# Block sums behind the low parts of probabilities, a wider spread of two of the sums, and one FFN sum on VectorE

## The chip, the core and the metric

The kernel runs on one core of a Trainium2 chip. TensorE (PE) multiplies matrices, VectorE (DVE), ScalarE (ACT) and GpSimd (POOL) work on tiles element by element, and SyncE (SP) issues the transfers between memory (HBM) and the core's SBUF. The metric is the device time of one execution in microseconds (us); less is better.

## The reference, cut to what matters

A decoder trunk of two layers on a sequence of 1024 tokens of 1024 numbers, in fp32:

```python
for l in range(DEPTH):                      # 2
    h = rmsnorm(x, norm1[l])
    p = h @ w_in[l]                         # q, k, v of both mixers, and two gates
    a = dilated_mixture(...)                # windows 128, 512, 2048 at dilations 1, 4, 16
    b = stick_breaking_attention(...)
    x = x + merge(a, b, gates, w_br[l]) @ w_o[l]
    h = rmsnorm(x, norm2[l])
    g, v = split(h @ w_up[l])               # 2816 + 2816 columns
    x = x + (gelu(causal_depthwise_conv(g)) * v) @ w_down[l]
out = rmsnorm(x, norm_f)
```

For the nearest window (128, dilation 1), each block of 128 queries attends its own block of keys and the one ahead of it: scores, bias, row minimum, exponential, transposed probabilities, product with the values.

## The kernel before

An fp32 product is made of three TensorE products of rounded parts: high x high, low x high, high x low. `split` (L128) makes the two parts of a 128x512 tile: ACT casts it to the high part (L129), DVE subtracts that from the tile, which leaves the low part (L130). Every weight, every normalized input and every tile of probabilities goes through it, so L130 is a line of many tiles: `w_lo` (weights), `t_lo` (block sums), `hl` (inputs, and the fourth block sum), `p0l` (probabilities of the nearest window), `g` (FFN products that are spilled to HBM).

Projections of pairs of column groups are computed in seven block products in place of eight (`seven`, L902), a scheme of Strassen's kind. It needs four block sums of the normalized input, each of four 128x512 rows (i = 0 to 3), which `block_sums` (L911) makes once per layer. The third and the first sum are three POOL steps per row (`first`, L928 to L930), the second and the fourth two DVE steps per row (`further`, L937 and L938), the second going on from the first's tile and the fourth from the second's. `in_two` then splits a row into its parts: `t_hi` and `t_lo`, and for the fourth sum `hh` and `hl`, which take the place of the input's quarter (0, 0). All sums of a row use one buffer, `h_sum` (the third's first two rows have another), so POOL may write a row of the first sum only when that row of the third has been split. The weights of a unit of seven products (`in_a`) get four POOL steps of their own (L1031, L1034, L1037, L1038) and are then split too. Within a unit PE takes the products in the order second sum, first sum, third sum, the input itself, fourth sum, into the banks i_a and i_c, which DVE drains (L1051 to L1077).

PE's order is written by hand. `attend` (L312) goes through the attention work and calls `dense.advance` between its pieces, which lays projections between them and takes one step from the list `dense.side` (`aside`); the block sums' steps are in that list, each with names of work that must be done first (`plan`). A first unit of seven products empties the list when it starts (in `step`). The nearest window's work per item is `score` (z, L591 and L708, exponential L709), `turn` (transposes t, L717, then `parts`, which splits the probabilities with a raised priority) and `apply` (products o, L729, then `fold`, L606). DVE, ACT and POOL each take their instructions in an order that a scheduler derived from the sequence in which the code issues them, with priority for what stands under `tc.high_priority`. Each engine runs its queue strictly in order.

In the FFN, `gated` (L1377ff) works on pairs of column groups: the product of gate and value is in the tiles cv (c, c12, s1, c21). POOL forms three differences for an odd j (L1382), and `spill` splits a tile and writes it to HBM (`g`, L1408). cv, the weights `up_a` (L1495) and others share buffers, so a weight's load waits until a spilled tile has been split for the last time.

## Time and profile before

| | |
|---|---|
| runs | 2699.85, 2701.89, 2702.15 us; median 2701.89 |
| profiled execution | 2703.52 us, span 2701.8 us |
| PE busy | 2650.5 us, 98% of the span |
| DVE, ACT, POOL busy | 2115.7, 1314.3, 734.9 us |
| mean granted clock of PE | 0.996 |
| stage 225 to 345 us (nearest window, layer one) | PE 114.1, DVE 99.0, ACT 70.4, POOL 42.7 us busy of 120 |
| same in layer two, 1572 to 1692 us | PE 114.7, DVE 98.9, ACT 66.9, POOL 45.3 us busy of 120 |

A row of a timeline gives the start, the duration of one group of like instructions (xN: N of them), the engine, the line and the tile written <- the tile read; in brackets at its end stands how long the engine was idle ahead of it and what released it. A row of waits gives the engine, the tile and line that waited, what it waited for, the sum in us, how many, and the longest. Instructions in a row start before the last one's end is shown, so a run of 0.68 us steps begins one every 0.60 us.

### The profile page before, as it was taken

The numbers are of one execution on the slowest core, as the hardware profiler recorded it, in microseconds if no ns is written. First come the engines' busy times: TensorE is split into PE (matmuls) and PEld (weight loads), VectorE is DVE, ScalarE is ACT, GpSimd is POOL, SyncE is SP. The second block draws the span as 40 slices with busy tenths as digits, with TensorE's granted clock in tenths as the row PEclk, the third lists the DMA queues.
The fourth block names the chain that finished last, engine by engine and source line by source line (L and its number), as shares of the span: only waits on it lengthen the run. The fifth ranks groups of instructions, "written<-read, shape, count | busy, mean of one in ns | idle before, by whom it ended". The sixth has DMA issues, their size and how long they took to land. (4 is left out here: it accounts for less than half of the span.)

```text
span 2701.8 us, 37158 instructions
## 1 busy us (share of the span) xinstructions
PE 2650.5 (98%) x13098; PEld 2226.4 (82%) x13098; DVE 2115.7 (78%) x3170; ACT 1314.3 (49%) x2434; POOL 734.9 (27%) x531
## 2 busy tenths in 40 slices
PE   8999999999999999999999999999999999999999
PEld 7888888888888888888889878888788888888888
DVE  5888876675789988897658887766858888998865
ACT  5656544364455555432335655434635555554225
POOL 2004133222233434321120042332311433343210
PEclk9999999999999999999999999999999999999999
DMA  4134489863235444688401334988732443447963
GB/s 153 28 97 125 132 239 234 205 229 118 82 117 172 141 156 143 222 325 313 167 32 48 102 120 145 254 208 226 234 90 75 151 160 135 170 144 254 333 246 121
DMA packets 399559, 448.88 MB, mean 166 GB/s; under 512 B 22044, under 2 KB 319372, under 8 KB 397836
## 3 DMA queue, kind: packets, MB, share of 16 engines
q1 hardware_dynamic: 399372, 446.49, 51.9%
q8 instruction: 104, 1.70, 0.3%
q14 instruction: 83, 0.68, 0.1%
HBM read 300.61 MB, written 142.67 MB: 164 GB/s over the span
## 5 line engine op out<-in xcount | busy, mean ns | idle before, releaser
L130 DVE TENSOR_TENSOR w_lo<-up_a,w_hi 128x512 fp32r<-128x512 f32 x240 | 236.9, 993 | 22.5 <-ACT w_hi L129 22.5
L129 ACT CAST w_hi<-up_a 128x512 fp32r<-128x512 f32 x240 | 149.4, 623 | 186.0 <-PE u_a L906 45.8
L1651 DVE TENSOR_TENSOR x<-x,d_ps 128x512 f32<-128x512 f32 (+1 forms) x228 | 152.3, 672 | 78.0 <-PE d_ps L1645 77.0
L1382 POOL TENSOR_TENSOR cv<-cv 128x512 f32<-128x512 f32 x88 | 131.9, 1509 | 249.0 <-DVE cv L1377 139.1
L130 DVE TENSOR_TENSOR w_lo<-w_raw,w_hi 128x512 fp32r<-128x512 f32 x176 | 133.9, 763 | 64.9 <-ACT w_hi L129 62.3
L129 ACT CAST w_hi<-w_raw 128x512 fp32r<-128x512 f32 x176 | 109.1, 621 | 130.1 <-PE o_ps L156 60.2
L129 ACT CAST w_hi<-in_a 128x512 fp32r<-128x512 f32 x140 | 86.8, 620 | 148.8 <-PE i_a L906 83.4
L130 DVE TENSOR_TENSOR g<-cv,g 128x512 fp32r<-128x512 f32 x154 | 152.3, 990 | 5.2 <-ACT g L129 2.8
L1643 PE MATMUL d_ps<-gd_in,w_hi 128*128 128x512 f32 (+1 forms) x340 | 130.2, 383 | 1.5 <-ACT w_hi L129 1.2
L1645 PE MATMUL d_ps<-gd_in,w_lo 128*128 128x512 f32 (+1 forms) x340 | 129.8, 382 | 0.0
L1644 PE MATMUL d_ps<-gd_in,w_hi 128*128 128x512 f32 (+1 forms) x340 | 129.7, 382 | 0.0
L905 PE MATMUL u_a<-hh,w_hi 128*128 128x512 f32 x320 | 124.7, 390 | 2.7 <-DVE u L1533 2.7
L906 PE MATMUL u_a<-t_lo,w_hi 128*128 128x512 f32 x320 | 124.5, 389 | 0.0
L907 PE MATMUL u_a<-hh,w_lo 128*128 128x512 f32 x320 | 124.5, 389 | 0.0
L905 PE MATMUL u_a<-t_hi,w_hi 128*128 128x512 f32 x320 | 124.5, 389 | 0.0
L906 PE MATMUL u_a<-hl,w_hi 128*128 128x512 f32 x320 | 124.5, 389 | 0.0
L907 PE MATMUL u_a<-t_hi,w_lo 128*128 128x512 f32 x320 | 124.5, 389 | 0.0
L130 DVE TENSOR_TENSOR w_lo<-in_a,w_hi 128x512 fp32r<-128x512 f32 x140 | 115.6, 826 | 3.8 <-ACT w_hi L129 3.5
L1038 POOL TENSOR_TENSOR in_a<-in_a 128x512 f32<-128x512 f32 x28 | 38.0, 1357 | 281.3 <-DVE w_lo L130 281.3
L1643 PE MATMUL d_ps<-gd_in,wd 128*128 128x512 f32 (+1 forms) x292 | 113.9, 390 | 0.0
L129 ACT CAST g<-cv 128x512 fp32r<-128x512 f32 x154 | 94.9, 616 | 38.1 <-POOL cv L1382 29.3
L1645 PE MATMUL d_ps<-gd_in,wd 128*128 128x512 f32 (+1 forms) x292 | 112.8, 386 | 0.0
(395 smaller groups left out, 8706.3 us busy)
## 6 DMA issues: line engine op xcount, KB each, us to landing
gd<-g SPq DMA_DIRECT2D x154, 512.0 KB, 3.6
gd_in<-gd SPq DMA_DIRECT2D x154, 512.0 KB, 6.2
up_a<-in_w_up_dram SPq DMA_DIRECT2D x80, 512.0 KB, 5.7
in_a<-in_w_in_dram SPq DMA_DIRECT2D x56, 512.0 KB, 5.4
w_raw<-in_w_in_dram SPq DMA_DIRECT2D x104, 256.0 KB, 3.4
t_kq<-tk SPq DMA_DIRECT2D x64, 384.0 KB, 7.6
wd_raw<-in_w_down_dram SPq DMA_DIRECT2D x22, 1024.0 KB, 8.0
gin<-gs SPq DMA_DIRECT2D x32, 512.0 KB, 5.2
```

The costliest lines, as they stand in the source:

```text
L129: act.copy(hi, src)
L130: dve.tensor_tensor(lo, src, f32(hi), ALU.subtract)
L905: pe.matmul(o, w[0][:, c], rh, start=(first and i == 0), stop=False, skip_group_check=True)
L906: pe.matmul(o, w[0][:, c], rl, start=False, stop=False, skip_group_check=True)
L907: pe.matmul(o, w[1][:, c], rh, start=False, stop=(last and i == 3), skip_group_check=True)
L1038: pool.tensor_tensor(a11, a22, a11, ALU.subtract)
L1382: return lambda: pool.tensor_tensor(dst, a, b, ALU.subtract)
L1643: pe.matmul(o[:, sub], wh[:, c], gh[:, sub], start=(i == 0 and k in (0, 4, 5)), stop=False, skip_group_check=True)
L1644: pe.matmul(o[:, sub], wh[:, c], gl[:, sub], start=False, stop=False, skip_group_check=True)
L1645: pe.matmul(o[:, sub], wl[:, c], gh[:, sub], start=False, stop=(i == m - 1), skip_group_check=True)
L1651: dve.tensor_tensor(x, x, o[:, sub], ALU.add)
```

## The change

`split` returns its DVE instruction, and `parts` keeps the latest one (the low part of probabilities) in `mark["low"]`. `behind()` puts the scheduler's place for what is issued within it after that instruction; `further` and `in_two` use it, so the DVE steps of the second and fourth sums and all splits of sums are placed behind the low part that was the latest when they were issued.

The second sum's steps are laid between the first's: row i of the first at 6i with its split at 6i + 7, the second's step at 6i + 8 and its split at 6i + 10, all from the point N01s on; before, they came one after another from N11s on. The fourth sum's step of row i was at i and its split at i + 1; now they are at 2i and 2i + 1, one per turn, and they are exempt from the emptying of the list when the first unit starts; what is left of them is now taken just ahead of the unit's fifth product.

In the FFN's first pair (j = 1) the differences come in the order s1, c12; the third, c = c21 - s1, is made by DVE in place of POOL, after the spill of c, and the spills of s1 and c12 change places.

```diff
     def split(hi, lo, src):
         act.copy(hi, src)
-        dve.tensor_tensor(lo, src, f32(hi), ALU.subtract)
+        return dve.tensor_tensor(lo, src, f32(hi), ALU.subtract)
+
+    mark = {}
+
+    def behind():
+        return tc.issue_after(mark["low"]) if mark else contextlib.nullcontext()
...
                     if self.now[2] and not self.started:
-                        while self.side:
+                        while self.side and self.side[0][0] != LAST_SUM:
...
         with tc.high_priority(offset=AHEAD):
-            split(hi[:, :n], lo[:, :n], src[:, :n])
+            mark["low"] = split(hi[:, :n], lo[:, :n], src[:, :n]).ins
...
-            dve.tensor_tensor(r, f32(ah), r, ALU.subtract)
-            dve.tensor_tensor(r, r, f32(al), ALU.add)
+            with behind():
+                dve.tensor_tensor(r, f32(ah), r, ALU.subtract)
+                dve.tensor_tensor(r, r, f32(al), ALU.add)
...
-            split(*S[t][i], at(t, i))
+            with behind():
+                split(*S[t][i], at(t, i))
...
-        series({"N01s"}, 1, lambda i: first(1, b12, b11, i), 7, 6)
-        series({"N11s"}, 2, lambda i: further(2, b22, i), 1, 1)
-        series({"plain", "01", "v0"}, 4, lambda i: further(4, b21, i), 1, 1)
+        steps = {}
+        for i in range(4):
+            for k, f in (
+                (0, lambda i=i: first(1, b12, b11, i)),
+                (7, lambda i=i: in_two(1, i)),
+                (8, lambda i=i: further(2, b22, i)),
+                (10, lambda i=i: in_two(2, i)),
+            ):
+                steps.setdefault(6 * i + k, []).append(f)
+        plan({"N01s"}, steps)
+        steps = {}
+        for i in range(4):
+            steps.setdefault(2 * i, []).append(lambda i=i: further(4, b21, i))
+            steps.setdefault(2 * i + 1, []).append(lambda i=i: in_two(4, i))
+        plan(LAST_SUM, steps)
...
             yield "turn"
             yield
+            while dense.side:
+                dense.aside()
             for word in seven(pa, w4, S[4], False, True):
...
-                at(1, less(c12, c, c12))
-                at(1, less(s1, c, s1))
+                pairs = [(2, c12), (1, s1)]
+                if j == 1:
+                    pairs.reverse()
+                for _, t in pairs:
+                    at(1, less(t, c, t))
                 at(later[0], lambda: spill(j, 6, c))
-                at(later[1], lambda: spill(j, 2, c12))
-
-                at(later[1], less(c, c21, s1))
-                at(later[2], lambda: spill(j, 1, s1))
+                if j > 1:
+                    at(later[1], lambda: spill(j, *pairs[0]))
+                at(later[1], less(c, c21, s1, dve if j == 1 else pool))
+                if j == 1:
+                    at(later[1], lambda: spill(j, *pairs[0]))
+                at(later[2], lambda: spill(j, *pairs[1]))
```

What this makes of the queues, by the order of the two programs (line numbers of the changed kernel are higher: L130 is L133 there, L543 and L544 are L551 and L552, L606 is L614, L937 and L938 are L946 and L947, L928 to L930 are L936 to L938, L1031 to L1038 are L1046 to L1053, and the numbers behind t_ and p_ differ a little). DVE in the second of the nearest window's items, before:

```order
L130 TENSOR_TENSOR t_lo<-h_sum,t_hi 128x512 x2
L130 TENSOR_TENSOR p0l<-t_2899,p0h 128x128
L130 TENSOR_TENSOR w_lo<-w_raw,w_hi 128x512
L130 TENSOR_TENSOR t_lo<-h_sum,t_hi 128x512 x2
L937 TENSOR_TENSOR h_sum<-hh_108,h_sum 128x512 x2
L130 TENSOR_TENSOR w_lo<-w_raw,w_hi 128x512
L938 TENSOR_TENSOR h_sum<-h_sum,hl_109 128x512
L130 TENSOR_TENSOR p0l<-t_2927,p0h 128x512
L606 TENSOR_TENSOR on<-o_2886,fold 64x512
L543 SCALAR_TENSOR_TENSOR ql<-q_ps,qt 64x512
```

and after:

```order
L133 TENSOR_TENSOR p0l<-t_2870,p0h 128x512
L133 TENSOR_TENSOR t_lo<-h_sum,t_hi 128x512
L551 SCALAR_TENSOR_TENSOR ql<-q_ps,qt 64x512
L552 SCALAR_TENSOR_TENSOR ql<-q_ps,qt 64x512
L133 TENSOR_TENSOR w_lo<-w_raw,w_hi 128x512
L133 TENSOR_TENSOR p0l<-t_2899,p0h 128x128
L133 TENSOR_TENSOR w_lo<-w_raw,w_hi 128x512
L133 TENSOR_TENSOR p0l<-t_2927,p0h 128x512
L551 SCALAR_TENSOR_TENSOR ql<-q_ps,qt 64x512
L614 TENSOR_TENSOR on<-o_2886,fold 64x512
```

Four t_lo, two L937 and an L938 stood between the p0l of t_2870 and that of t_2927; one t_lo is left, and the others come later. POOL at the end of the first sum, before:

```order
L928 TENSOR_TENSOR h_sum<-hl_109,hl_363 128x512
L929 TENSOR_TENSOR h_sum<-h_sum,hh_108 128x512
L928 TENSOR_TENSOR h_sum<-hl_109,hl_363 128x512
L930 TENSOR_TENSOR h_sum<-h_sum,hh_362 128x512
L929 TENSOR_TENSOR h_sum<-h_sum,hh_108 128x512
L930 TENSOR_TENSOR h_sum<-h_sum,hh_362 128x512
L1031 TENSOR_TENSOR in_a<-in_a 128x512
L1034 TENSOR_TENSOR in_a<-in_a 128x512
L1037 TENSOR_TENSOR in_a<-in_a 128x512
L1038 TENSOR_TENSOR in_a<-in_a 128x512
```

and after:

```order
L936 TENSOR_TENSOR h_sum<-hl_109,hl_363 128x512
L937 TENSOR_TENSOR h_sum<-h_sum,hh_108 128x512
L938 TENSOR_TENSOR h_sum<-h_sum,hh_362 128x512
L1046 TENSOR_TENSOR in_a<-in_a 128x512
L1049 TENSOR_TENSOR in_a<-in_a 128x512
L1052 TENSOR_TENSOR in_a<-in_a 128x512
L936 TENSOR_TENSOR h_sum<-hl_109,hl_363 128x512
L937 TENSOR_TENSOR h_sum<-h_sum,hh_108 128x512
L938 TENSOR_TENSOR h_sum<-h_sum,hh_362 128x512
L1053 TENSOR_TENSOR in_a<-in_a 128x512
```

The three weight steps (L1046, L1049, L1052) now stand ahead of the first sum's last row. ACT in the same place, before (the four t_hi are the first sum's rows):

```order
L129 CAST t_hi<-h_sum 128x512 x4
L129 CAST p0h<-t_2899 128x128
L129 CAST w_hi<-w_raw 128x512 x2
L538 ACTIVATE qt<-q_ps 64x512
L129 CAST p0h<-t_2927 128x512
L538 ACTIVATE qt<-q_ps 64x512
L605 COPY fold<-o_2886 64x512
L129 CAST p0h<-t_2962 128x384
L129 CAST w_hi<-w_raw 128x512
L1000 COPY q1s<-r_ps 128x512
L129 CAST p0h<-t_2995 128x384
```

and after:

```order
L132 CAST t_hi<-h_sum 128x512 x2
L132 CAST w_hi<-w_raw 128x512
L132 CAST p0h<-t_2899 128x128
L132 CAST t_hi<-h_sum 128x512
L132 CAST w_hi<-w_raw 128x512
L546 ACTIVATE qt<-q_ps 64x512
L132 CAST p0h<-t_2927 128x512
L546 ACTIVATE qt<-q_ps 64x512
L613 COPY fold<-o_2886 64x512
```

The cast of the first sum's row 2 (the t_hi that stands alone) is now ahead of the high part p0h of t_2927; the cast of row 3 follows after p0h of t_2995 and ahead of that of t_3039. DVE in the first unit of seven products, from the p0l that was at 326.21 us in the trace, before:

```order
L130 TENSOR_TENSOR p0l<-t_3560,p0h 128x384
L938 TENSOR_TENSOR h_sum<-h_sum,hl_363 128x512
L1051 TENSOR_TENSOR u<-u,i_a 128x512
L606 TENSOR_TENSOR on<-o_3511,fold 64x512
L130 TENSOR_TENSOR hl_109<-h_sum,hh_108 128x512
L130 TENSOR_TENSOR w_lo<-in_a,w_hi 128x512
L130 TENSOR_TENSOR p0l<-t_3593,p0h 128x512
L793 TENSOR_SCALAR bias_4241<-base_78 128x256
L794 TENSOR_SCALAR bias_4241<-base_79 128x256
L1056 TENSOR_TENSOR u_3551<-u,i_c 128x512
```

and after, up to the last low part of the fourth sum (hl written from h_sum):

```order
L133 TENSOR_TENSOR w_lo<-in_a,w_hi 128x512
L133 TENSOR_TENSOR hl_109<-h_sum,hh_108 128x512
L947 TENSOR_TENSOR h_sum<-h_sum,hl_363 128x512
L1079 TENSOR_TENSOR u_3535<-u_3535,i_a 128x512
L614 TENSOR_TENSOR on<-o_3592,fold 64x512
L133 TENSOR_TENSOR hl_109<-h_sum,hh_108 128x512
L946 TENSOR_TENSOR h_sum<-hh_362,h_sum 128x512
L133 TENSOR_TENSOR w_lo<-in_a,w_hi 128x512
L947 TENSOR_TENSOR h_sum<-h_sum,hl_363 128x512
L1084 TENSOR_TENSOR u<-u,i_c 128x512
L133 TENSOR_TENSOR w_lo<-in_a,w_hi 128x512
L133 TENSOR_TENSOR hl_109<-h_sum,hh_108 128x512
```

The second half of the fourth sum (L946, L947, hl) stands between the drains of the unit (L1079, L1084), where before the last hl was ahead of the second drain (L1056). From the p0l of the same transposes (t_3544 in the changed kernel) to the last hl are 24 rows there, of which these are the last 12.

DVE in the first FFN pair, before:

```order
L130 TENSOR_TENSOR w_lo<-up_a,w_hi 128x512
L130 TENSOR_TENSOR g<-cv,g 128x512
L130 TENSOR_TENSOR w_lo<-u,w_hi 128x512
L130 TENSOR_TENSOR g<-cv,g 128x512 x2
L130 TENSOR_TENSOR w_lo<-up_a,w_hi 128x512
L130 TENSOR_TENSOR g<-cv,g 128x512
```

and after:

```order
L133 TENSOR_TENSOR w_lo<-up_a,w_hi 128x512
L133 TENSOR_TENSOR g<-cv,g 128x512
L133 TENSOR_TENSOR w_lo<-u,w_hi 128x512
L1399 TENSOR_TENSOR cv<-cv 128x512
L133 TENSOR_TENSOR g<-cv,g 128x512 x2
L133 TENSOR_TENSOR w_lo<-up_a,w_hi 128x512
```

One step, the sum of L1399, is added ahead of the two splits; on POOL the group `L1382 ... cv<-cv 128x512 x3` has become x2.

More of the change, by code (lines that the diff above doesn't have):

```diff
@@ L951, in plan @@
                 todo.append((after, lambda fs=steps.get(k, ()): [g() for g in fs]))
-        def series(after, t, f, lag, gap):
-            steps = {}
-            for i in range(4):
-                steps.setdefault(i * gap, []).append(lambda i=i: f(i))
-                steps.setdefault(i * gap + lag, []).append(lambda i=i: in_two(t, i))
-            plan(after, steps)
         def third(i):
@@ L1379, in gated, with less @@
             later = (2, 3, 4, 5, 7) if j == 1 else (3, 5, 7, 9, 11) if j == NF - 1 else (1, 4, 7, 11, 14)
[L1381 to L1382 removed]
+            def less(dst, a, b, eng=pool):
+                return lambda: eng.tensor_tensor(dst, a, b, ALU.subtract)
             if j % 2 == 0:
```

4 lines of the change are left out of this document (2 added, 2 removed).

## The prediction

> **What bounds the kernel now.** I began with the page's busy times, went on to TensorE's waits summed by what releases them, and then to the timeline around each wait.
>
> ```profile
> PE 2650.5 (98%) x13098; PEld 2226.4 (82%) x13098; DVE 2115.7 (78%) x3170; ACT 1314.3 (49%) x2434; POOL 734.9 (27%) x531
> PE o L729 <- DVE p0l L130: 10.6, 8, 3.1
> PE u_a L905 <- DVE u L1533: 2.7, 2, 1.6
> ```
>
> TensorE (PE) is busy in 2650.5 of 2701.8 us. The change leaves its instructions and their order as they are, so it can only take away or add idle time of PE. Two groups of waits touch the code that changes: eight waits, 10.6 us in all, for the low part p0l of probabilities, and two, 2.7 us, for an FFN weight. Together 13.3 us, 0.5%. Everything it could gain is in there. The timeline of PE gives the waits of the first layer, and the wait view cut to the same stage of each layer says that they come twice alike:
>
> ```profile
> 265.82 0.33 PE L729 MATMUL o<-p0l,v 128*128 128x128 f32 x1 [1.28 <-DVE p0l L130]
> 272.49 0.38 PE L729 MATMUL o<-p0l,v 128*128 128x256 f32 x1 [3.06 <-DVE p0l L130]
> 326.80 0.33 PE L729 MATMUL o<-p0l,v 128*128 128x128 f32 x1 [0.71 <-DVE p0l L130]
> 330.64 0.38 PE L729 MATMUL o<-p0l,v 128*128 128x256 f32 x1 [0.23 <-DVE p0l L130]
> PE o L729 <- DVE p0l L130: 5.3, 4, 3.1
> ```
>
> 1.28 + 3.06 + 0.71 + 0.23 = 5.28 us per layer. I follow the first layer and count it twice. What VectorE (DVE) did just ahead of the two long ones:
>
> ```profile
> 263.01 2.43 DVE L130 TENSOR_TENSOR t_lo<-h_sum,t_hi 128x512 fp32r<-128x512 f32 x2
> 265.47 0.29 DVE L130 TENSOR_TENSOR p0l<-t,p0h 128x128 fp32r<-128x128 f32 x1
> 265.68 1.45 DVE L130 TENSOR_TENSOR w_lo<-w_raw,w_hi 128x512 fp32r<-128x512 f32 x1
> 267.05 2.37 DVE L130 TENSOR_TENSOR t_lo<-h_sum,t_hi 128x512 fp32r<-128x512 f32 x2
> 269.35 1.28 DVE L937 TENSOR_TENSOR h_sum<-hh,h_sum 128x512 f32<-128x512 f32 x2
> 270.55 0.68 DVE L130 TENSOR_TENSOR w_lo<-w_raw,w_hi 128x512 fp32r<-128x512 f32 x1
> 271.15 0.68 DVE L938 TENSOR_TENSOR h_sum<-h_sum,hl 128x512 f32<-128x512 f32 x1
> 271.75 0.68 DVE L130 TENSOR_TENSOR p0l<-t,p0h 128x512 fp32r<-128x512 f32 x1
> ```
>
> The block sums' steps (t_lo, L937, L938) fill the queue without a break while p0l stands behind them. A 128x512 step alone is shown as 0.68 and follows the last at 0.60 (270.55, 271.15, 271.75). The same step takes longer where GpSimd (POOL) computes:
>
> ```profile
> 315.22 3.48 DVE L938 TENSOR_TENSOR h_sum<-h_sum,hl 128x512 f32<-128x512 f32 x2
> 318.62 0.68 DVE L130 TENSOR_TENSOR p0l<-t,p0h 128x512 fp32r<-128x512 f32 x1
> 336.31 1.54 DVE L130 TENSOR_TENSOR w_lo<-in_a,w_hi 128x512 fp32r<-128x512 f32 x1
> 315.08 1.36 POOL L1031 TENSOR_TENSOR in_a<-in_a 128x512 f32<-128x512 f32 x1 [0.34 <-DMA in_a<-in_w_in_dram]
> 316.52 1.62 POOL L1034 TENSOR_TENSOR in_a<-in_a 128x512 f32<-128x512 f32 x1
> 318.23 1.63 POOL L1037 TENSOR_TENSOR in_a<-in_a 128x512 f32<-128x512 f32 x1
> ```
>
> Two steps took 3.48, 1.74 each, so 1.14 more than the pitch of 0.60; a w_lo in the next such stretch took 1.54, 0.86 more than 0.68. The p0l beside POOL's third step (318.62), which reads PSUM, took no more than usual. So what a block-sum step costs depends on what POOL does at that moment.
>
> **The change part by part.**
>
> *The low parts go ahead.* In the new order the p0l of 265.47 has one t_lo ahead of it in place of two and stands behind queries' two steps and a w_lo; its high part was ready at 264.16 (ACT's 263.89 + 0.27, quoted below). I replay the queue to an end of about 263.95 on the shifted times and take the 1.28 as gone. Of the second wait, the six block-sum steps from 267.05 (2.37 + 1.28 + 0.60, about 4.2 us with the w_lo's left in place) no longer stand there, which is more than 3.06: on DVE alone this wait goes as well.
>
> What is late next is on POOL and ScalarE (ACT). The third sum's low parts now stand behind p0l too, and the first sum is made by POOL in the same buffer, row by row, once the third sum's row has been split.
>
> ```profile
> 261.92 1.30 POOL L930 TENSOR_TENSOR h_sum<-h_sum,hh 128x512 f32<-128x512 f32 x1
> 261.58 2.28 ACT L129 CAST t_hi<-h_sum 128x512 fp32r<-128x512 f32 x4
> 263.89 0.27 ACT L129 CAST p0h<-t 128x128 fp32r<-128x128 f32 x1
> 278.52 0.59 ACT L129 CAST p0h<-t 128x512 fp32r<-128x512 f32 x1 [1.28 <-PE t L717]
> 281.82 0.39 PE L729 MATMUL o<-p0l,v 128*128 128x256 f32 x1
> ```
>
> Before, POOL ended the first sum at 263.2 and ACT then split four parts in a row. Now row 2 can start on POOL only when its third-sum row is split, at about 261, and needs three steps of about 1.3: about 265.1. ACT's cast of it (0.57) stands ahead of the cast for the second wait's p0l; with a w_hi, a queries' cast and p0h at about 0.6 each behind it, p0l ends near 268.6, where PE, 1.28 ahead of before, wants it at 268.15: a wait of 0.45 in place of 3.06. Row 3 comes after POOL's three weight steps and after a third-sum split that DVE now does at about 271: POOL ends it near 275.5, and ACT's cast of it blocks the cast of the next p0h of 512 columns but one. That p0h then ends about 277.95 and its p0l about 278.75; PE, 3.9 ahead of before (1.28 + 3.06 - 0.45), wants it at 281.82 - 3.9 = 277.9: a new wait of 0.87 (bounds 0, were POOL to reach row 3 earlier, and 1.7, two DVE steps more). So far 0.45 + 0.87 - 4.34 = -3.0 us per layer.
>
> *The second sum between the first's.* Its steps are the same in number (16 per layer) and lie in the stretch where DVE has room; the last low part now lands in the first unit. I cost that inside the next part, since PE's later demand for the fourth sum absorbs a wait before it.
>
> *The fourth sum spread.* This is the largest price. Before, two of its steps already ran at 315.22, and its last low part ended at 329.38. Now all twelve steps stand behind the p0l that ended at 326.75, between the drains of the first unit.
>
> ```profile
> 326.21 0.54 DVE L130 TENSOR_TENSOR p0l<-t,p0h 128x384 fp32r<-128x384 f32 x1
> 328.69 0.69 DVE L130 TENSOR_TENSOR hl<-h_sum,hh 128x512 fp32r<-128x512 f32 x1
> 338.23 0.40 PE L906 MATMUL i_a<-hl,w_hi 128*128 128x512 f32 x1
> 332.55 1.29 POOL L1038 TENSOR_TENSOR in_a<-in_a 128x512 f32<-128x512 f32 x1 [12.70 <-DVE w_lo L130]
> 336.00 1.29 POOL L1031 TENSOR_TENSOR in_a<-in_a 128x512 f32<-128x512 f32 x1 [2.17 <-DMA in_a<-in_w_in_dram]
> 337.37 1.63 POOL L1034 TENSOR_TENSOR in_a<-in_a 128x512 f32<-128x512 f32 x1
> 339.08 1.29 POOL L1037 TENSOR_TENSOR in_a<-in_a 128x512 f32<-128x512 f32 x1
> 330.13 1.01 SPq L1020 DMA_DIRECT2D in_a<-in_w_in_dram  x2
> ```
>
> Ahead of that p0l stand, in the new order, four such steps fewer and two short bias steps more (some 0.4 together), so it ends about 2.0 earlier, 324.75. From it to the last low part of the fourth sum are 24 instructions: 24 x 0.60 = 14.4, so 339.2 at the earliest; PE reads that part at 338.23. Without any slowing PE is 1.0 late. But the next unit's load (330.13 in the queue of SP, right behind the last w_lo of this unit's first pieces) is issued about 1.4 earlier with that w_lo, and lands near 334 or 335 in place of 336.0, so POOL's four steps, 1.29 + 1.29 + 1.63 + 1.29 = 5.5 us, fall between 332.4 and 339: where DVE does the second half of the fourth sum. In such a stretch I count two block-sum steps at +1.14 and one w_lo at +0.86, 3.1 us. The sum is 4.1 late on this clock. The bounds: 1.0 with no slowing, and below it 0 if drains let DVE run ahead (and then the 0.94 of the last two p0l waits comes off as well, -0.94); above, 6.9 when four steps each wait for a POOL step of mean 1.46 (1.0 + 4 x 1.46). I take 4.1, since the rows at 315.22 and 336.31 show exactly this pairing of steps. The 0.94 of the waits at 326.80 and 330.64 is inside the 338.23 and so inside these 4.1.
>
> The Trainium skill, "SBUF — State Buffer", section "SBUF: two separate sides", says that a DVE step with two SBUF inputs and a GpSimd step that reads SBUF hold a shared port exclusively, the loser blocked for the other's whole instruction, where the row shows +1.14 beside POOL steps of 1.36 to 1.63; by that rule at four meetings the upper bound above would be the forecast. "GPSIMD Engine Reference", section "Specifications", counts only DVE steps with two SBUF inputs or in a 2-port mode as sharing, and by that rule the unslowed p0l at 318.62 agrees.
>
> *The FFN sum on DVE.* It is one step more on DVE and one fewer on POOL per layer.
>
> ```profile
> 768.02 1.61 POOL L1382 TENSOR_TENSOR cv<-cv 128x512 f32<-128x512 f32 x1 [0.70 <-DVE g L130]
> 768.40 2.38 DVE L130 TENSOR_TENSOR g<-cv,g 128x512 fp32r<-128x512 f32 x2
> 770.84 1.25 SPq L1495 DMA_DIRECT2D up_a<-in_w_up_dram  x2
> 776.39 0.62 ACT L129 CAST w_hi<-up_a 128x512 fp32r<-128x512 f32 x1 [5.19 <-DMA up_a<-in_w_up_dram]
> 778.48 0.47 PE L905 MATMUL u_a<-hh,w_hi 128*128 128x512 f32 x1 [1.13 <-DVE u L1533]
> ```
>
> The load that PE ends up waiting for is issued at 770.84, as soon as the second of the two g splits (768.40 to 770.78) has read the buffer. While POOL's step runs beside them they take 2.38; without it they take 1.28, but DVE does the sum first, +0.60 to 0.68. Net 2.38 - 1.28 - 0.60 = 0.5 earlier, on a path (load, cast, low part, u) that ends in PE's wait of 1.13; in layer two the wait is larger, so the whole 0.5 counts there too. Gain 0.5 per layer, 1.0 in all (bounds 0 and 2.7).
>
> **The sum.** Per layer -3.0 + 4.1 = +1.1; two layers +2.2; FFN -1.0: +1.2 us. Against the profiled execution's own time (2703.52, its span 2701.8 and 1.7 around it) that is 2704.7; this execution stands 1.6 above the median of the runs shown, 2701.89, so as a time I give 2703.1.
>
> **The rivals.** (A) The fourth sum is in time: POOL's steps do not meet it, or DVE gets further ahead than 0.60 per row allows in my count, and the 0.94 goes as well: 2 x (-3.0 - 0.94) - 1.0 = -8.9, 2693.0. For it: DVE is only 78% busy, and I count every row from 324.75 on as back to back. Against it: 24 rows and a margin that is negative even without slowing. With no slowing but these rows, 2 x (-3.0 + 1.0) - 1.0 = -5.0, 2696.9. (B) All ten waits vanish with nothing in their place: -13.3, 2688.6. Against it stand the buffer that holds POOL back and ACT's fixed order. (C) Slower: POOL and DVE block each other step for step while the fourth sum is made. With four steps at a whole POOL step each, 2 x (-3.0 + 6.9) - 1.0 = +6.8, 2708.7. It decides once PE's last fourth-sum read is more than 6.2 late (2 x 3.2 - 1.0 = 5.4), a low part written after about 344.4 on the clock of before. For it: the 3.48 for two, and w_lo's of the next unit, which stand in the same queue. (D) The FFN part does nothing, since the earlier load meets other transfers: 2704.1, no other verdict.
>
> **How the numbers follow.** 0.2% of the time is 5.4 us, about what a measurement of this kernel can tell from no change: 2696.5 and 2707.3 are the borders. Forecast with (D) and the case of no slowing: 0.54, nearly all within 0.2%. (A) 0.23 and (B) 0.04, with 0.02 from the edge of the forecast: faster 0.29. (C) 0.19, of which 0.17 is beyond the border: slower 0.17, the rest same 0.54. The range goes from (A)'s 2693.0 to (C)'s 2708.7, which leaves out (B) and the far tails of both.
>
> **What the profile after would show.** Right: the p0l waits of 1.28 and 3.06 are gone, with short ones for p0l behind ACT's t_hi; POOL's last row of the first sum stands behind three weight steps; PE waits at the first unit's last product for hl, some 3 to 5 us less what it gained; the load at 770.84 is issued about 0.5 earlier. Wrong: no wait for hl, which means that I overcounted DVE's queue or POOL's meeting with it (A); a wait for hl of more than 6 us, or block-sum steps of two us and more (C); a wait for a score or a bias (z) that grows, which I have not counted.

## The result, and the profile after

The changed kernel takes 2708.55 us (median) where the kernel before takes 2701.67 in the same comparison: a ratio of 1.0027, 95% interval 1.0017 to 1.0036. It is slower by 6.9 us. Measured once more later, beside other kernels, it took 2710.17 against 2702.61: 1.0031, 1.0019 to 1.0043. The forecast was 2703.1, within 0.2% of no change; the result lies in the range (2693.0 to 2708.7), at the upper end of it, where rival (C) stood. In the table below s4_back and before_filled each have one execution of over 5000 us, which is left out of their medians and ratios.

The first part of the changed kernel's page, and its view of PE's waits in the stage from 225 to 345 us (engine, tile and line that waited, what for: total, times, longest):

```profile
PE 2657.0 (98%) x13098; PEld 2229.3 (82%) x13098; DVE 2102.1 (78%) x3172; ACT 1313.9 (49%) x2434; POOL 735.0 (27%) x529
PE i_a L913 <- ACT hh L132: 3.8, 1, 3.8
PE r_ps L163 <- DVE ql L552: 1.9, 1, 1.9
PE o L737 <- ACT p0h L132: 0.4, 1, 0.4
PE i_a L914 <- DVE hl L133: 0.4, 1, 0.4
PE o L737 <- DVE p0l L133: 0.3, 1, 0.3
PE i_a L914 <- DVE t_lo L133: 0.3, 1, 0.3
```

Two things are to be seen. The four waits for p0l, 5.3 us, have shrunk to 0.7 (with p0h), and in their place stand 1.9 for ql and 4.1 for the fourth sum's parts hh and hl. And PE is *busy* 6.5 us longer than before (2657.0 against 2650.5) with the same 13098 instructions. Waits alone do not show that: it must be in the length of the products. The timeline of PE around the long wait shows where:

```profile
335.17 0.40 PE L914 MATMUL i_a<-hl,w_hi 128*128 128x512 f32 x1
335.41 0.39 PE L915 MATMUL i_a<-hh,w_lo 128*128 128x512 f32 x1
339.57 0.79 PE L913 MATMUL i_a<-hh,w_hi 128*128 128x512 f32 x1 [3.77 <-ACT hh L132]
340.72 0.80 PE L914 MATMUL i_a<-hl,w_hi 128*128 128x512 f32 x1 [0.36 <-DVE hl L133]
...
341.74 0.63 PE L913 MATMUL i_a<-t_hi,w_hi 128*128 128x512 f32 x1
342.16 0.63 PE L914 MATMUL i_a<-t_lo,w_hi 128*128 128x512 f32 x1
...
345.56 0.40 PE L914 MATMUL i_a<-t_lo,w_hi 128*128 128x512 f32 x1
345.80 0.40 PE L915 MATMUL i_a<-t_hi,w_lo 128*128 128x512 f32 x1
```

Behind the wait a 128x512 product takes 0.63 and begins every 0.43 us, until 345.5 us; before and after that it takes 0.40 and begins every 0.23. The view of the same kernel by stretches (start and end, length, busy time with the number of instructions for PE, weight loads, DVE, ACT, POOL, then the granted clock of PE as a share of full speed, the DMA engines' share and GB/s) says what that is:

```profile
338.70:345.50 6.80, 5.58 (x14) 4.18 (x15) 3.92 (x8) 1.89 (x5) 0.00 (x0) 0.50 0.27 76
270.00:273.00 3.00, 2.97 (x10) 2.37 (x10) 1.21 (x2) 0.00 (x0) 2.17 (x2) 0.57 0.40 132
```

The granted clock is 0.50 for 6.8 us behind the long wait. Behind the wait for ql it is 0.50 for 3.4 us, from 270.44 to 273.85; the second row, which begins a little earlier, shows a mean of 0.57. The Trainium skill, "TensorE: Matmul & The Clock Gate", Part 1, describes a gate that halves PE's clock after an idle window of about 3.4 us of a free-running grid; by that the stretches of 3.4 us and twice that agree. That it takes a whole idle window does not agree: the wait for ql is 1.88, with 0.73 of waits just ahead of it. In the 3.41 us ahead of 338.71 PE was busy for 0.49, in those ahead of 270.44 for 1.19.

What the stage costs can be read by taking one product in both timelines. In the kernel before:

```profile
264.21 0.33 PE L729 MATMUL o<-p0h,v 128*128 128x128 f32 x1
276.04 0.28 PE L729 MATMUL o<-p0h,v 128*128 128x256 f32 x1
337.54 0.39 PE L906 MATMUL i_a<-hl,w_hi 128*128 128x512 f32 x1
340.73 0.40 PE L906 MATMUL i_a<-t_lo,w_hi 128*128 128x512 f32 x1
```

and the same four in the changed kernel, the last two of them shown above at 335.17 and 345.56:

```profile
262.84 0.30 PE L737 MATMUL o<-p0h,v 128*128 128x128 f32 x1
274.79 0.28 PE L737 MATMUL o<-p0h,v 128*128 128x256 f32 x1
```

The differences (after less before) are -1.37, -1.25, -2.37 and +4.83. The two early waits, 1.28 and 3.06, both lie between the first and the second of these products, so their places together give nothing (from -1.37 to -1.25). The two small p0l waits are gained (-1.1), and the fourth sum costs 7.2: 3.77 + 0.36 of waits, and 3.07 of products at half clock. Layer two repeats it (a wait for hh of 3.75, and +7.0 at the same place). Over both layers the changed kernel's profile loses 11.5 us in these stages against that of before; 6.2 it gets back, most of it near 421 and 1759 us, where the profile of before has a half-clock stretch each and that of the changed kernel has none.

### The profile page after: what moved, and what is told of

It reads as the page before. It is cut to its first block, busy times and chain, and to the rows that moved or that the text cites. A ratio compares the mean times of both kernels' runs of the same rounds, so it can differ in the third digit from the quotient of the medians.

```text
span 2707.1 us, 37172 instructions
## 1 busy us (share of the span) xinstructions
PE 2657.0 (98%) x13098; PEld 2229.3 (82%) x13098; DVE 2102.1 (78%) x3172; ACT 1313.9 (49%) x2434; POOL 735.0 (27%) x529
## 5 line engine op out<-in xcount | busy, mean ns | idle before, releaser
L133 DVE TENSOR_TENSOR w_lo<-up_a,w_hi 128x512 fp32r<-128x512 f32 x240 | 237.8, 997 | 20.0 <-ACT w_hi L132 20.0
L1399 POOL TENSOR_TENSOR cv<-cv 128x512 f32<-128x512 f32 x86 | 129.1, 1513 | 246.9 <-DVE cv L1394 131.8
L133 DVE TENSOR_TENSOR w_lo<-w_raw,w_hi 128x512 fp32r<-128x512 f32 x176 | 134.9, 769 | 67.7 <-ACT w_hi L132 64.9
L133 DVE TENSOR_TENSOR g<-cv,g 128x512 fp32r<-128x512 f32 x154 | 150.3, 977 | 5.2 <-ACT g L132 2.7
L133 DVE TENSOR_TENSOR w_lo<-in_a,w_hi 128x512 fp32r<-128x512 f32 x140 | 113.4, 810 | 5.0 <-ACT w_hi L132 4.6
L1053 POOL TENSOR_TENSOR in_a<-in_a 128x512 f32<-128x512 f32 x28 | 39.4, 1408 | 274.5 <-DVE w_lo L133 274.5
```

Of the source, the lines that this page charges most:

```text
L133: return dve.tensor_tensor(lo, src, f32(hi), ALU.subtract)
L1053: pool.tensor_tensor(a11, a22, a11, ALU.subtract)
L1399: return lambda: eng.tensor_tensor(dst, a, b, ALU.subtract)
```

## The experiments

All are timed against the kernel before in the same comparison; the interval is the 95% interval of the ratio. What is called the stage's cost is the difference of one product's place in two timelines, as above.

| kernel | median, us | before, us | ratio | interval |
|---|---|---|---|---|
| s4_back | 2705.59 | 2702.02 | 1.0013 | 1.0004 to 1.0022 |
| third_free | 2708.94 | 2702.02 | 1.0023 | 1.0013 to 1.0033 |
| both_back | 2704.88 | 2702.02 | 1.0013 | 1.0005 to 1.0022 |
| ffn_alone | 2703.22 | 2702.02 | 1.0008 | 0.9999 to 1.0016 |
| s4_filled | 2708.13 | 2702.44 | 1.0023 | 1.0013 to 1.0033 |
| late_load | 2709.82 | 2702.44 | 1.0030 | 1.0018 to 1.0041 |
| before_filled | 2701.74 | 2702.44 | 0.9999 | 0.9990 to 1.0008 |
| both_filled | 2703.20 | 2702.44 | 1.0005 | 0.9996 to 1.0014 |
| no_pool | 2701.89 | 2702.67 | 0.9997 | 0.9989 to 1.0006 |
| near_only | 2722.51 | 2702.67 | 1.0077 | 1.0063 to 1.0091 |
| near_filled | 2719.58 | 2702.67 | 1.0067 | 1.0054 to 1.0080 |
| s4_alone | 2710.15 | 2702.67 | 1.0032 | 1.0020 to 1.0045 |
| s4_close | 2704.00 | 2702.61 | 1.0010 | 1.0002 to 1.0019 |
| s4_close_filled | 2701.74 | 2702.61 | 0.9999 | 0.9990 to 1.0008 |
| s4_spread_free | 2701.07 | 2702.61 | 0.9995 | 0.9986 to 1.0004 |
| after_again | 2710.17 | 2702.61 | 1.0031 | 1.0019 to 1.0043 |
| free_filled | 2701.81 | 2702.32 | 1.0000 | 0.9992 to 1.0009 |
| free_filled2 | 2701.46 | 2702.32 | 0.9999 | 0.9990 to 1.0008 |

### Which part brings the loss

The fourth sum's part alone, on the kernel before:

```diff
-                        while self.side:
+                        while self.side and self.side[0][0] != LAST_SUM:
...
+            with behind() if t == 4 else contextlib.nullcontext():
                 dve.tensor_tensor(r, f32(ah), r, ALU.subtract)
...
-        series({"plain", "01", "v0"}, 4, lambda i: further(4, b21, i), 1, 1)
+            steps.setdefault(2 * i, []).append(lambda i=i: further(4, b21, i))
+            steps.setdefault(2 * i + 1, []).append(lambda i=i: in_two(4, i))
```

(The same condition stands at the split in `in_two`, and what is left of the fourth sum is taken ahead of the unit's fifth product, as in the change.)

> The kernel before, with the fourth sum's part alone: spread, behind the low parts, not taken when the first unit starts. Theory: this part by itself brings the whole loss, 5 to 7 us per layer less the 0.9 of the two small waits: 2711 to 2715. Rival: the loss needs the second sum's later steps on DVE as well; alone the fourth sum is about 2 us (four rows) earlier and the wait and its slow stretch are smaller: 2704 to 2707.

2710.15: the whole loss. Its PE waits in the stage:

```profile
PE o L737 <- DVE p0l L133: 4.4, 2, 3.1
PE i_a L913 <- ACT hh L132: 3.2, 1, 3.2
PE i_a L914 <- DVE hl L133: 0.6, 1, 0.6
```

The two early p0l waits (1.28, 3.07) are as before, and 3.84 for the fourth sum has come. So the rival, that it needs the second sum's later steps as well, falls.

The other way round, the fourth sum as before in the changed kernel:

```diff
-                        while self.side and self.side[0][0] != LAST_SUM:
+                        while self.side:
...
-            steps.setdefault(2 * i, []).append(lambda i=i: further(4, b21, i))
-            steps.setdefault(2 * i + 1, []).append(lambda i=i: in_two(4, i))
+            steps.setdefault(i, []).append(lambda i=i: further(4, b21, i))
+            steps.setdefault(i + 1, []).append(lambda i=i: in_two(4, i))
```

(and `behind()` for t other than 4 only).

> The changed kernel with the fourth sum as before: taken when the first unit starts, a row per turn, not behind the low parts. Theory A: the changed kernel loses its time at the fourth sum, per layer 3.77 + 0.36 us of PE waits for hh and hl and then 6.8 us at half the granted clock (3.41 lost). Then 7.5 us per layer come off, 15 in all, less up to 1.9 if the two small p0l waits (0.71, 0.23) return: 2693.5 to 2695.5. Rival B: only the waits cost, and the slower clock is made up elsewhere: 8.3 less 1.9, so 2702. Rival C: the time is lost near 267 to 274 us, where the first sum's rows come late: not faster than 2706.

2705.59, not 2694. The wait for hh and hl is gone, but others have come into the first unit of the first layer: 0.62 for t_hi, 1.12 for t_lo (the second sum's last row, which the change makes later) and 1.74 for a drain u, behind the fourth sum's steps that now crowd in front. The time is about that of rival C, but not its place: the new waits end at 322.8, 324.5 and 331.2 us, not near 267 to 274. Two of my three theories treated the fourth sum as separable from the second; it is not, they share DVE's rows at that place.

A question remains on the fourth sum: is it the spread or the place behind p0l that makes it late? With the spread kept and only `behind()` taken off for t = 4 (in `further` and `in_two`):

```diff
-            with behind():
+            with behind() if t != 4 else contextlib.nullcontext():
```

> The changed kernel with the fourth sum spread as there but not behind the low parts: tells which of the two, the spread or the order behind p0l, makes the last low part late. By the order its last hl stands 5 rows earlier than in the changed kernel. If the order behind p0l is the cause: the wait falls from 4.1 to about 1 and less contention, 2700 to 2702. If the spread is the cause: it stays above 2705.

2701.07, 7 to 9 us less than the changed kernel. The waits of PE in the stage:

```profile
PE r_ps L163 <- DVE ql L552: 1.9, 1, 1.9
PE i_a L914 <- DVE t_lo L133: 1.1, 1, 1.1
PE i_a L913 <- ACT t_hi L132: 0.6, 1, 0.6
```

and the last of the fourth sum, which ended at 340.67 in the changed kernel:

```profile
336.05 0.94 DVE L133 TENSOR_TENSOR hl<-h_sum,hh 128x512 fp32r<-128x512 f32 x1
```

No wait for hh or hl is left. So with the spread kept, the fourth sum is late only if it also stands behind the low parts. With the order kept and the rows closer (the second diff above without its first half):

> The changed kernel with one thing changed: the fourth sum's step and split of row i at i and i + 1 in place of 2i and 2i + 1 (still exempt from the emptying, still behind the low parts). In the order its last low part then stands 11 rows earlier than in the changed kernel, and ahead of POOL's weight steps. Theory: no wait for hh and hl and no slow stretch there, while the near stage keeps its gain (0.4) and the two small p0l waits stay away (1.0): per layer 1.4 less than before, with 0.4 to 1 from the FFN: 2698.5 to 2699.5, faster than both kernels. Rival: a low part p0l now stands behind the fourth sum's steps and 0.5 to 1 us of waits return: 2701. Rival: the whole loss is from the near stage's slow stretches, 2706.

2704.00: the wait for hl is gone here too, and 1.1 for p0h and 0.26 for p0l have come near 333 us. So it takes both, the order and the spread, to make the fourth sum late; the question as I put it, which of the two, was wrong. This version beats the changed kernel and not the one before; the forecast of 2699 counted a gain near 270 us that is not there.

### POOL beside DVE

The four steps of POOL beside the fourth sum left out, so that two units have weights that lack these steps and only the time is read:

```diff
+            S["unit"] = unit = S.get("unit", 9) + 1
-            pool.tensor_tensor(a21, a21, a22, ALU.add)
+            if unit != 3:
+                pool.tensor_tensor(a21, a21, a22, ALU.add)
...
+            if unit != 2:
                 pool.tensor_tensor(a11, a22, a11, ALU.subtract)
```

> The changed kernel, with four of POOL's weight steps per layer left out: the fourth of the second unit and the first three of the third, which are those that run at 330.9 to 337.7 us beside the fourth sum (the weights of these two units are then not the right ones; times alone are read). Contention theory: the three DVE steps of 1.62, 1.77 and 1.74 us go back to 0.68, the wait of 4.1 for hh and hl falls to about 1.0, and no slow stretch of the clock follows: 6.2 us less per layer or, counting the whole stage's +7.2 against +1, 2 x 6 = 12 less: 2696.5. Rival: the 24 DVE rows set it and POOL's share is small: 2706 or more.

2701.89. In the changed kernel three DVE steps ran beside POOL's:

```profile
333.28 1.62 DVE L133 TENSOR_TENSOR hl<-h_sum,hh 128x512 fp32r<-128x512 f32 x1
334.82 1.77 DVE L946 TENSOR_TENSOR h_sum<-hh,h_sum 128x512 f32<-128x512 f32 x1
336.52 1.74 DVE L133 TENSOR_TENSOR w_lo<-in_a,w_hi 128x512 fp32r<-128x512 f32 x1
333.05 1.30 POOL L1046 TENSOR_TENSOR in_a<-in_a 128x512 f32<-128x512 f32 x1
334.43 1.62 POOL L1049 TENSOR_TENSOR in_a<-in_a 128x512 f32<-128x512 f32 x1
336.12 1.59 POOL L1052 TENSOR_TENSOR in_a<-in_a 128x512 f32<-128x512 f32 x1
```

Without them:

```profile
333.61 0.69 DVE L133 TENSOR_TENSOR hl<-h_sum,hh 128x512 fp32r<-128x512 f32 x1
334.22 0.68 DVE L947 TENSOR_TENSOR h_sum<-hh,h_sum 128x512 f32<-128x512 f32 x1
334.82 0.68 DVE L133 TENSOR_TENSOR w_lo<-in_a,w_hi 128x512 fp32r<-128x512 f32 x1
PE i_a L913 <- ACT hh L132: 0.7, 1, 0.7
PE i_a L914 <- DVE hl L133: 0.6, 1, 0.6
```

The three steps are 5.13 - 2.05 = 3.1 us shorter, and PE's wait falls from 4.13 to 1.33, by 2.8. No half-clock stretch follows, and the stage costs 1.9 where it cost 7.2. This is the contention shown in its size. The rows above also show its form: POOL's three steps end at 334.35, 336.05 and 337.71, and the DVE steps that began beside them at 334.90, 336.59 and 338.26, each 0.54 or 0.55 later, about the pitch of one step alone. They look as if each DVE step did its work only when POOL's step was over. An attempt to move POOL's steps by their load missed:

```diff
+            fresh = S.pop("fresh", None)
-            if dense.loads:
+            if dense.loads and not fresh:
                 dense.loads.pop(0)()
             dense.last(0)
...
+            if dense.loads and fresh:
+                dense.loads.pop(0)()
             while dense.side:
                 dense.aside()
```

> The changed kernel with the load of the next weights issued later in the first unit, just ahead of the fourth sum's product, so that POOL's four weight steps fall behind the fourth sum. Contention theory: three DVE steps there cost 0.94 + 1.09 + 1.06 = 3.1 us more than their usual 0.68; without it the wait of 4.1 falls to about 1.0 and no slow stretch follows: 2 x (3.1 + 3.4) = 13 less, 2695.5. Rival: the number of DVE rows alone sets it (24 x 0.60), the wait stays: 2708. Against both: the next unit's weights come late and PE waits there instead, up to 3 us per layer.

2709.82. The load of the weights in question is issued at 326.44 us, as in the changed kernel (326.48), so the place of the call did not set its time; POOL's steps stand where they stood, and the run says nothing of either theory.

### The half clock

Four products by zeros (they add nothing to the bank) into the long wait of the changed kernel:

```diff
+            for _ in range(idle if i == 3 else 0):
+                pe.matmul(o, zero.to_broadcast([P, P]), f32(b[0][0]), start=False, stop=False, skip_group_check=True)
```

> The changed kernel with four products by a tile of zeros (fp32, 128x512, about 0.85 us each) laid into PE's wait ahead of the fourth sum's last row in the first unit; they add zero to the bank. Nothing on DVE, ACT or POOL moves, so hh and hl come when they came. Clock theory: a stretch of 3.4 us in which PE is active less than about half is followed by a stretch of 3.4 us at half clock; with PE kept active both slow stretches per layer go (3.41 us lost each): 2708.5 - 6.8 = 2701.7, the wait itself still there as zeros. Rival (PE's longer products come from something else, such as transfers or POOL at that time): no change, 2708.5, or later by the zeros that overrun.

The stretch behind it in this kernel's view by stretches:

```profile
339.60:345.20 5.60, 4.64 (x21) 3.62 (x22) 4.06 (x9) 2.47 (x7) 0.00 (x0) 1.00 0.32 94
```

against the changed kernel:

```profile
339.60:345.20 5.60, 5.24 (x14) 3.87 (x15) 3.02 (x6) 1.08 (x3) 0.00 (x0) 0.50 0.28 78
```

The clock stays at 1.00 and 21 products pass in 5.6 us in place of 14; in layer two the half clock is gone as well. That PE's inactivity brings the half clock behind the long wait is shown. The stage costs 5.0 in place of 7.2, and in layer two 5.0 in place of 7.0. But the median is 2708.13, only 0.4 less than the changed kernel's, where 2.2 + 2.0 = 4.2 was due by the stages; the intervals of the two ratios allow 4 and also nothing. In this profile other half-clock stretches stand near 424 and 1765 us, which the changed kernel's profile lacks. By the products' places each costs 1.6 there, and the wait ahead of the second is 1.05 longer (1.68 against 0.63). The second profile of the changed kernel was taken to see that:

> The changed kernel once more, for a second profile of the same program at another place of the clock's stretches. Clock theory: the same waits (0.39, 0.34, 1.88; 3.77, 0.36 per layer), slow stretches after the long one always, after the shorter group and at the other two or three places (near 421 and 1759 us in the profile of before) sometimes; time 2707 to 2710. Rival: slow stretches at the same places each time.

Its waits for p0h, p0l, ql, hh and hl are those of the first profile to within 0.06 us, and the long wait is again followed by 6.8 us at half clock, but a stretch that the first profile lacks has come:

```profile
338.20:345.00 6.80, 4.96 (x12) 3.57 (x13) 4.54 (x9) 1.78 (x4) 0.00 (x0) 0.50 0.19 54
427.00:430.40 3.40, 3.40 (x13) 2.71 (x12) 1.73 (x7) 1.60 (x6) 0.00 (x0) 0.50 1.06 227
```

The wait of 3.7 to 3.8 us for hh was followed by 6.8 us at half clock in both layers of all four profiles that have it with nothing laid into it (the changed kernel's two, late_load and third_free). A shorter wait does not always bring it: PE's wait for a score (z) of 1.45 us was followed by a half-clock stretch near 424 us in s4_filled and by none at the same place in the changed kernel's first profile. What decides that, the place of the wait on the grid for one, no run here tests.

The same filling in the kernel before, in its wait of 3.06 (five products of 128x256):

> The kernel before with five products by zeros (fp32, 128x256, about 0.43 us each) in the wait of 3.06 us for p0l. Clock theory: in the profiled execution that wait fell across two stretches and no slow one followed, but the stretches are not tied to the program; in most executions one follows, so up to 2 x 1.71 come off: 2698.5 to 2700.5. Rival: as in that profile, the wait has no second price: 2702.

2701.74: no clear difference. And ahead of the wait for ql, in two versions without the fourth sum's lateness and in the one with both parts undone (all with the same edit, at the end of `apply` for the second item; free_filled2 has one more product by zeros in the first unit's first product):

```diff
+            if (pr, s, i) == (0, 1, (0, 0)):
+                for _ in range(3):
+                    pe.matmul(o[:, 0:256], zero.to_broadcast([P, P]), f32(shared[i][0][:, 0:256]), start=False, stop=False, skip_group_check=True)
```

> The same with three products by zeros (0.43 us each) ahead of the wait for ql near 270 us. Clock theory: one slow stretch per layer less in most executions, 1.5 us each: 2 to 3 us less than without them, 2696 to 2697. Rival: no difference, as in the kernel before with its wait filled.

> The kernel with both undone (fourth sum as before, third sum's splits not behind; measured 2704.9), with three products by zeros (0.43 us each) ahead of the wait of 1.85 us for ql that stands where p0l's 3.06 was. Clock theory: one slow stretch per layer less in most executions: 2701.5. Rival: the slow stretches there are not the reason for its 2704.9: no change.

> The changed kernel with the fourth sum spread but not behind the low parts (measured 2701.1), and three products by zeros (0.43 us each) ahead of the wait for ql near 270 us. Clock theory: the slow stretch after that wait goes in most executions, as with the fourth sum closer (2704.0 to 2701.7): about 2.3 less, 2698.8, faster than both kernels by about 0.1%. Rival: no difference, 2701.

> The same, with one product by zeros (0.85 us) also in the first unit's first product, ahead of the wait of 1.12 us for t_lo, where a slow stretch followed in one layer of the profile. Clock theory: another 0.5 to 1.5 less, 2697.5 to 2698.5. Rival: the zeros run past the wait and cost what they save.

s4_close_filled: 2701.74 against 2704.00, as forecast in size, with intervals against the kernel before that overlap. both_filled: 2703.20 against 2704.88, from two comparisons. free_filled and free_filled2: 2701.81 and 2701.46 against 2701.07, no gain, although free_filled2's profile records no half-clock stretch at all ahead of the last 4 us. So the half clock behind short waits could not be shown in the time. None of these versions is faster than the kernel before.

### The near stage, and the rest

The third sum's splits not behind p0l (`behind()` in `in_two` for t other than 3):

> The changed kernel, but the splits of the third sum are not placed behind the low parts, so POOL may write the first sum's rows 2 and 3 earlier. Theory: the late rows cause, per layer, PE waits of 0.39 + 0.34 + 1.88 us and one window at half clock (1.71 lost), 4.3 in all; all of it goes, 8.6 for two layers: 2700. If one third-sum split ahead of p0l brings back the old wait of 1.28: 2702.5. Rival: the first sum's own splits stand behind p0l and ACT still waits for POOL, nothing changes: 2708.

2708.94: no change. PE's wait for p0h and p0l (0.39 + 0.34) becomes one of 0.60 for p0l, and the 1.85 for ql stays. My theory that POOL's late rows cause the ql wait falls; they cause 0.1 us. With the fourth sum as before besides:

> Both undone: fourth sum as before, third sum's splits not behind; left are the first and second sums behind the low parts, the second between the first's, and the FFN part. If the two losses are independent: 2708.6 - 15 - 8.6 = 2685, with the small p0l waits back 2687. Rival: the freed DVE steps crowd the p0l again and the waits of 1.28 and 3.06 return in part: 2693 or more.

2704.88, where 2685 to 2687 was expected and the rival said 2693 or more. PE's waits in the stage of this kernel:

```profile
PE r_ps L163 <- DVE ql L552: 1.9, 1, 1.9
PE i_a L914 <- DVE t_lo L133: 1.1, 1, 1.1
PE o L737 <- DVE p0l L133: 1.1, 2, 0.6
PE i_a L913 <- ACT t_hi L132: 0.6, 1, 0.6
```

4.7 us of waits where the kernel before has 5.3. The order behind the low parts frees p0l and finds the next thing late: ql, and the second sum. How late the second sum can become shows the kernel before with the first sum's splits and the second sum's steps behind p0l and nothing else:

```diff
+            with behind() if t == 2 else contextlib.nullcontext():
                 dve.tensor_tensor(r, f32(ah), r, ALU.subtract)
...
+            with behind() if t in (1, 2) else contextlib.nullcontext():
                 split(*S[t][i], at(t, i))
```

> The kernel before, with only the first sum's splits and the second sum's steps placed behind the low parts; no interleaving, fourth sum and FFN as before. Theory: the wait of 1.28 goes and that of 3.06 becomes 0.6 + 1.85 (p0l, then ql), 1.7 to 1.9 us less per layer, and the later waits stay as before: 2702 - 3.5 = 2698.5. Rival: the second sum, now later, makes t_hi and t_lo late at the first unit (0.6 + 1.1 per layer, as where the fourth sum alone was undone): 2702.

> The same with three products by zeros (fp32, 128x256, 0.43 us each) ahead of the wait for ql. Clock theory: PE stays active there and the stretch of half clock that follows that place in most executions goes: 1 to 3 us less than without them. Rival: no difference.

2722.51 and 2719.58. PE waits for t_hi, t_lo and a drain of the first unit, and the clock is at half from 322 to 336:

```profile
PE i_a L913 <- DVE t_lo L132: 2.6, 4, 1.4
PE i_a L912 <- ACT t_hi L131: 1.7, 1, 1.7
PE i_a L912 <- DVE u L1060: 1.3, 1, 1.3
322.00:337.00 15.00, 12.19 (x32) 7.74 (x33) 13.24 (x22) 5.35 (x11) 0.00 (x0) 0.54 0.04 17
```

both_back, at 2704.88, differs from near_only by the interleaving of the second sum and by the FFN part, which gives nothing alone. So the interleaving is what makes the order behind p0l bearable.

The FFN's part alone:

> The kernel before with the FFN part alone (first pair's third difference on DVE, spills exchanged). By the two profiles PE's waits there went from 2.7 to 1.3 us in all: -1.4, so 2700.3; the prediction said -1.0. Rival: nothing, 2701.7.

2703.22: no gain. The load is issued earlier (770.65 in a timeline that runs 0.36 later there, so 0.5 earlier, as forecast), and PE's wait is 2.7 in all as before: the transfer took about 6.05 us from its issue to the cast that it releases, where it had taken 5.55. Single profiles do not settle why: in the two profiles of the changed kernel the same load took 4.60 and 6.33, and PE's wait for it was 0.5 and 1.4.

## Why the prediction was right or wrong

*The first step.* "So it can only take away or add idle time of PE" was the first thing wrong, and the rest of the sum stands on it. PE ran the same products in the same order, but was busy 6.5 us longer, at half clock behind its waits. No term of the sum had a place for that.

*The two early p0l waits.* The gain of 1.28 came. For the second wait the replay said 0.45 in place of 3.06, and 0.39 + 0.34 stood there. The late rows of the first sum on POOL were as replayed (row 2 ended at 264.6 us, forecast 265.1; row 3 at 275.1, forecast 275.5), but the wait of 0.87 that I hung on row 3 (0.83 by its own figures) did not come: PE, slowed at another place, wanted its p0l later. What failed here is "so far 0.45 + 0.87 - 4.34 = -3.0": I looked only at what the moved steps delay and not at what PE meets next once it is early. That was the product into r_ps, which waited until DVE had done the second of the ql steps: 1.88, and 1.7 at half clock behind it. In the changed kernel:

```profile
269.19 0.69 DVE L552 SCALAR_TENSOR_TENSOR ql<-q_ps,qt 64x512 fp32r<-64x512 f32 x1
270.03 0.47 PE L163 MATMUL r_ps<-hh,w_hi 128*128 128x512 f32 x1 [1.88 <-DVE ql L552]
```

and the same two in the kernel before:

```profile
272.94 0.40 PE L155 MATMUL r_ps<-hh,w_hi 128*128 128x512 f32 x1
274.11 0.69 DVE L544 SCALAR_TENSOR_TENSOR ql<-q_ps,qt 64x512 fp32r<-64x512 f32 x1
```

There the product did not wait for that step, which ended 1.9 us after the product had begun, so the long wait for p0l did not simply hide the wait for ql. That the product now stands in the bank that this step reads, and did not before, is argued from these rows and not shown. Measured at the products' places from the stage's start on: -0.3 in place of -3.0 per layer.

*The fourth sum.* PE's waits there are 4.13, but this is not the forecast's 4.1: that one counts from PE's place with the 0.94 of the two small p0l waits inside it. With the 1.1 that these gave, the waits make PE 4.13 - 1.1 = 3.0 late, and 1.33 - 1.1 = 0.2 without POOL, where 1.0 was forecast. The part of POOL's meeting was right: three DVE steps 3.1 us longer beside it (forecast 3.1). The load was issued at 326.48, 3.7 earlier than before and not 1.4, and POOL's four steps ran from 330.90 to 337.71 (forecast 332.4 to 339). What failed is that the wait was taken as the whole price. PE stood still long enough for the clock to be halved for 6.8 us, another 3.07 per layer. The term was 4.1 and measured 7.2 - 1.1 = 6.1, of which half is the clock.

*The FFN.* -1.0 was forecast, 0 measured; the earlier issue was there, the earlier landing was not. This is the time of rival (D); that the load met other transfers is not shown.

*The sum.* Forecast +1.2. By terms as measured, 2 x (-0.3 - 1.1 + 7.2) = +11.6 in the profiled executions of the two stages; the median moved by 6.9. What lies between is not settled: half-clock stretches elsewhere, 1.6 us each where measured, come in some profiles and not in others. Rival (C) gave 2708.7 for a lateness of 6.9; the time fits, but the lateness was 3.0 and as much again was the clock, so that the result lies in the range is luck. The 1.46 for a POOL step in (C) is also more than the mean of the four steps named (1.29, 1.29, 1.63, 1.29), 1.375; by that (C) and the top of the range would be 2707.9, below the measured time. DVE and POOL did block each other, but at three steps, and each time only for what was left of POOL's step (+0.94, +1.09 and +1.06 beside POOL's 1.30 to 1.62). That agrees with the rule of the Trainium skill, "SBUF — State Buffer", section "SBUF: two separate sides", that the prediction named: the 0.54 or 0.55 us from the end of POOL's step to that of DVE's, shown above, is what it would give. The prediction set the row against the rule because it took a whole POOL step for each meeting.

*What would show it.* The signs named for "right" were there: a wait for hl and hh of 3 to 5 us, POOL's last row behind the weight steps, and short p0h and p0l waits. I gave a wait of more than 6 us as the point for "slower"; 4.1 was enough. The point was set without the clock.

## What to carry to other kernels

A wait of PE is not over when it ends: one of 3.8 us was followed by 6.8 us at half clock and so cost 7.2 in place of 4.1, and a few waits close together brought 3.4 us of it. To put work behind what is waited for helps only as long as that work has room: here four rows of a sum got later, the last by 11 us, and met POOL, and to take off the order behind the low parts for the fourth sum alone gave back the whole loss. Before counting a wait as a gain, look for what PE needs next once it is early; here it was a step that DVE did four steps further on.

## What was not expected of the hardware

The half clock came behind a group of waits of 0.39, 0.34 and 1.88 us within 3.6 us; no single one of them is as long as a stretch. Behind one wait it does not always come: the 3.06 us in the profile of the kernel before had none behind it in either layer and the same wait in s4_alone had one in layer one only, while in the profile of ffn_alone it had one in each layer:

```profile
271.50:275.00 3.50, 3.25 (x9) 2.69 (x10) 3.44 (x7) 0.00 (x0) 0.00 (x0) 0.51 0.57 187
1613.00:1616.40 3.40, 3.40 (x11) 2.73 (x10) 3.34 (x6) 0.48 (x1) 0.00 (x0) 0.50 0.40 126
```

Products by zeros kept the clock up behind the long wait (s4_filled).

That three DVE steps beside three POOL steps cost 1.61 to 1.78 us each, where they cost 0.68 alone, was in the forecast, and held in the profiles of after_again, third_free, late_load, s4_filled and s4_alone. That a DVE step so met ends 0.54 or 0.55 us behind POOL's was not.
